# Hybrid attention layer on one core: the input turned by DMA transposes in place of fp32 transposes on TensorE

## The chip, the core and the metric

The kernel runs on one core of a Trainium2 chip. TensorE (PE in the profile) multiplies matrices, VectorE (DVE), ScalarE (ACT) and GpSimd (POOL) do elementwise work, and SyncE (SP) issues transfers to 16 DMA engines; ScalarE issues some as well. Every engine works through its own instructions in order. The metric is the time of one execution on the device in microseconds (us), lower is better.

## The reference

One decoder layer on 4096 tokens of width 1024, in fp32:

```
mod = silu(c) @ w_ada + b_ada;  shift, scale, gate = split(mod, 3)
h = rmsnorm(x, norm_g) * (1 + scale) + shift
proj = h @ w_in                       # 3328 columns, for two head groups
A: stick-breaking attention, 8 heads x 64, strictly causal, no softmax, SiLU gate
B: sliding window of 128, 8 query / 2 key-value heads x 64, ALiBi, sink logit, SiLU gate
x = x + gate * (concat(A, B) @ w_out);  out = rmsnorm(x, final_g)
```

## The kernel before

The tokens are taken in eight superblocks (s = 0 to 7) of 512, each of four blocks of 128. To keep fp32 accuracy with fp16 matmuls, every operand is split into a high and a low half, and every product takes three passes (high x high, high x low, low x high).

The normalised and modulated input of a superblock, hT, has the 1024 features on partitions, in eight groups k of 128, and the tokens as columns. A projection chunk (line 381) is 128 output columns for 512 tokens: 24 matmuls of 512 columns, written as four quarters of six. The values (lines 451 and 463) use hT as the stationary operand. In each superblock come first the sliding-window keys, four gates and four queries, the values, and the output projection of the superblock before (line 623); then, for each of four pairs of stick-breaking heads, chunks K, Q and G. The x items prepare hT of the next superblock while these twelve stick-breaking chunks run: x is loaded two blocks at a time, normalised (its square sum on ScalarE, line 304, the inverse root on GpSimd, the scaling on VectorE, line 309), and then turned on TensorE (`tr`, line 349): four items of four fp32 transposes into a PSUM buffer, evacuated by ScalarE with scale and shift (line 354), cast to the high half by VectorE (line 357), and the low half subtracted by GpSimd (line 358). The four PSUM buffers "mm" serve projections, output and these transposes in turn.

Attention runs in ticks laid between these items: a tick holds the scores z of a group of two query blocks and two heads (lines 493 to 500), or the products with the values, here called the value group (line 577) of the group two before. Between the two, ScalarE, VectorE and GpSimd make the weights (the stick-breaking scan is line 513), split them (lines 558 and 559), and SyncE turns them by DMA transposes (line 564). `gate` multiplies the result with the gate (line 593) and splits it (lines 594 and 595).

The order is written by hand. `main` fills a list of items with planned costs (1300 ns for a quarter), and each tick is placed by a due time worked out from these costs; `later(n, f)` runs f after n more items of TensorE's work. Items of cost 0 go between. In s = 0 the weights are loaded, split (lines 275 and 276) and written to DRAM for the later superblocks, and 22 extra items fold the gate into the output weights (lines 236 to 238), one after every second item.

Of the kernel before, what the change touches and what calls it, by code (L numbers as in the profile page):

```python
# [10 lines left out]
I32 = mybir.dt.int32  # L11
AF = mybir.ActivationFunctionType
# [4 lines left out]
D = 1024  # L17
# [19 lines left out]
class Ring:  # L37
    """n buffers of a tag, taken in turn"""
# [12 lines left out]
class Kern:  # L51
# [9 lines left out]
    def open_const(self, ctx):  # L61
# [66 lines left out]

    def mod_cols(self, which):
        nc = self.nc  # L130
        ps = self.P["pv"].tile([128, 512], F32, tag="pv", name="modps")
        for j in range(KD):
            nc.tensor.matmul(out=ps[:, j:j + 1], lhsT=self.fg[:, j * 128:(j + 1) * 128], rhs=self.ones[:, 0:1],
                             start=True, stop=True)
# [5 lines left out]
    def setup_x0(self):  # L140
        """modulation and the first superblock's input"""
# [7 lines left out]
        for t in xs[:2]:  # L149
            self.x_norm(t)  # L150
# [4 lines left out]
        for t in xs[2:]:  # L155
            self.x_norm(t)
# [18 lines left out]
        hT = self.hT[0] = self.P["hT"].tile([128, KD, 2, T], F16, tag="hT", name="hT")  # L175
        for k in range(KD):
            nc.scalar.activation(hT[:, k, 0, :], xT[:, k, :], AF.Identity, bias=self.s16[:, k:k + 1])
            nc.vector.scalar_tensor_tensor(out=hT[:, k, 1, :], in0=xT[:, k, :], scalar=self.s16[:, k:k + 1],
                                           in1=hT[:, k, 0, :], op0=ALU.add, op1=ALU.subtract)

    def setup_masks(self):
# [3 lines left out]
        rel = self.P["y32"].tile([128, 256], F32, tag="y32", name="rel")  # L185
# [7 lines left out]
        nc.gpsimd.memset(self.d1, 1.0)  # L193
        nc.gpsimd.affine_select(out=self.d1, in_=self.d1, pattern=[[0, 4], [1, 256]], compare_op=ALU.is_ge,
                                fill=0.0, base=-128, channel_multiplier=-1)

    def setup_wo_items(self):
        """gate folded into the output weights; every item loads for the one after next"""
# [15 lines left out]
        def bcast():  # L214
            gb = st["gb"] = self.fg
# [34 lines left out]
        return out + [(0.0, self.load_fg)]  # L250
# [77 lines left out]
    def x_items(self, s, row0):  # L328
# [8 lines left out]
        def norm(g):  # L337
            for b in (2 * g, 2 * g + 1):
                self.x_norm(st[b])
# [640 lines left out]
```

## Time and profile before

| | |
|---|---|
| time, median of 3 runs | 1821.07 us |
| lowest and highest | 1820.89 and 1821.63 us |
| span of the profiled execution | 1820.7 us |
| TensorE busy | 1711.4 us (94%) |
| VectorE, ScalarE, GpSimd busy | 1081.8, 768.6, 536.5 us |
| HBM read and written | 141.58 and 27.79 MB |

The span goes from the first to the last instruction of one profiled execution; it stands 0.4 us below the median time. Busy shares are means over the whole span. Matmuls are pipelined and their ends are modelled, so a TensorE shown as busy is not at its peak; the start times are what to compare.

### The profile page before, as it was taken

Reading aid. Unit: us, or ns where it says so; the run is one execution under the profiler, and the core shown is the slowest. Engines: PE = TensorE matmul, PEld = TensorE weight load, DVE = VectorE, ACT = ScalarE, POOL = GpSimd, SP = SyncE. Lnnn points to the kernel's source line nnn. Section 1 sums busy time; section 2 is a strip of 40 time slices with the busy share of each in tenths; the row PEclk is TensorE's granted clock in tenths of the full one; section 3 lists DMA queues with packets and bytes.
Section 4 is the critical chain, followed back from the end, with each engine's and each line's share of the span. In section 5 each row is a group of like instructions: output and inputs, shape, how many; then the busy total and the mean of one; then the engine's idle time right before and its main releaser. Section 6 shows DMA issues by size and latency. Waiting matters only on the chain.

```text
span 1820.7 us, 28484 instructions
## 1 busy us (share of the span) xinstructions
PE 1711.4 (94%) x10982; PEld 894.6 (49%) x10982; DVE 1081.8 (59%) x1888; ACT 768.6 (42%) x1476; POOL 536.5 (29%) x665
## 2 busy tenths in 40 slices
PE   3997689999999989999999999999899998999997
PEld 3453345444555444555455554545455544455443
DVE  5577872558635585365735567354863557546582
ACT  3544552445423453244524454243633445234441
POOL 2034440234312252133412343122531235212231
PEclk8998889999999999999999999999999999999999
DMA  8797652465526555256443565246552655426552
GB/s 288 215 243 198 182 157 72 116 170 160 135 54 145 172 151 135 59 151 188 132 99 91 146 187 143 59 125 187 143 147 56 141 172 144 127 64 152 154 118 85
DMA packets 361621, 257.85 MB, mean 142 GB/s; under 512 B 288604, under 2 KB 315268, under 8 KB 361476
## 3 DMA queue, kind: packets, MB, share of 16 engines
q1 hardware_dynamic: 340308, 178.86, 40.4%
q10 hardware_dynamic: 21168, 77.08, 12.6%
q8 instruction: 88, 1.44, 0.3%
q14 instruction: 57, 0.47, 0.1%
HBM read 141.58 MB, written 27.79 MB: 93 GB/s over the span
## 4 chain that ended last, share of the span: by engine, by line
PE 74%; DVE 14%; issue 4%; ACT 3%; POOL 2%; DMA 1%; ACTq 0%; DVEq 0%; POOLq 0%
PE mm L381 36%; PE mm L623 18%; PE mm L451 9%; PE pv L577 4%; PE z L500 3%; DVE nb L513 3%; PE mm L463 2%; DVE w L559 2%; DVE f L309 1%; DVE fg L124 1%; DVE beta L519 1%; POOL hT L358 1%; DMA wT<-w 1%; DVE w L276 1%; ACT w L558 1%
## 5 line engine op out<-in xcount | busy, mean ns | idle before, releaser
L381 PE MATMUL mm<-hT,w 128*128 128x512 f16 x4032 | 921.1, 384 | 9.7 <-ACT h L354 3.8
L381 PEld LDWEIGHTS <-w 128*128 128x128 f16 x4032 | 392.9, 99 | 471.3 <-issue 29.4
L623 PE MATMUL mm<-wo,yT 128*128 128x512 f16 x1536 | 347.1, 380 | 0.0
L549 POOL TENSOR_SCALAR p<-p,smm 128x256 f32<-128x256 f32 x256 | 122.5, 496 | 695.8 <-DVE smm L547 352.1
L623 PEld LDWEIGHTS <-yT 128*128 128x128 f16 x1536 | 148.6, 98 | 169.4 <-issue 1.3
L540 ACT ACTIVATE p<-sp,nm 128x256 f32<-128x256 f32 (+1 forms) x256 | 126.0, 493 | 214.1 <-DVE nm L533 214.1
L595 POOL TENSOR_TENSOR yT<-y,yT 128x256 f16<-128x256 f32 x128 | 144.5, 1129 | 235.9 <-DVE yT L594 200.3
L513 DVE TENSOR_TENSOR_SCAN nb<-nb,d 128x1024 f32<-128x1024 f32 x64 | 153.2, 2394 | 94.5 <-ACT nb L507 93.4
L509 POOL TENSOR_SCALAR_AFFINE_SELECT beta<-beta 128x512 f32<-128x512 f32 x64 | 108.3, 1692 | 242.1 <-ACT beta L508 242.1
L451 PE MATMUL mm<-wv,hT 128*128 128x512 f16 x768 | 172.5, 379 | 0.0
L533 DVE CUSTOM_DVE_ANT_0 sp<-z,bias,nsink 128x256 f32<-128x256 f32 (+1 forms) x256 | 107.3, 475 | 36.2 <-PE z L500 35.5
L559 DVE SCALAR_TENSOR_TENSOR w<-p,w 128x1024 f16<-128x1024 f32 x64 | 83.1, 1299 | 71.6 <-ACT w L558 71.6
L558 ACT ACTIVATE w<-beta 128x1024 f16<-128x1024 f32 x64 | 67.5, 1055 | 123.1 <-DVE beta L519 119.7
L451 PEld LDWEIGHTS <-hT 128*128 128x128 f16 x768 | 74.2, 98 | 84.3
L577 PEld LDWEIGHTS <-v 128*64 128x64 f16 x2304 | 89.0, 110 | 53.7 <-issue 49.8
L577 PE MATMUL pv<-wT,v 128*64 128x128 f16 (+1 forms) x2304 | 110.1, 240 | 1.8 <-DMA wT<-w 1.8
L507 ACT ACTIVATE nb<-z 128x1024 f32<-128x1024 f32 x64 | 65.4, 1022 | 98.7 <-PE z L500 73.2
L558 ACT ACTIVATE w<-p 128x1024 f16<-128x1024 f32 x64 | 67.6, 1057 | 83.4 <-POOL p L549 69.4
L304 ACT ACTIVATE junk<-f 128x1024 bf16<-128x1024 f32 x64 | 67.5, 1055 | 78.2 <-DVE f L629 63.8
L442 DVE SCALAR_TENSOR_TENSOR v<-mm,v 128x512 f16<-128x512 f32 (+1 forms) x64 | 31.3, 489 | 110.6 <-ACT v L441 109.0
L397 DVE SCALAR_TENSOR_TENSOR q<-mm,q 64x512 f16<-64x512 f32 x64 | 43.8, 684 | 80.1 <-ACT q L396 79.0
L559 DVE SCALAR_TENSOR_TENSOR w<-beta,w 128x1024 f16<-128x1024 f32 x64 | 83.0, 1297 | 6.6 <-ACT w L558 6.6
(105 smaller groups left out, 1727.8 us busy)
## 6 DMA issues: line engine op xcount, KB each, us to landing
w<-wsc ACTq DMA_DIRECT2D x147, 512.0 KB, 3.4
f<-in_x_dram SPq DMA_DIRECT2D x64, 512.0 KB, 3.9
q<-q SPq DMA_DIRECT2D x128, 128.0 KB, 2.6
out_dram<-f SPq DMA_DIRECT2D x32, 512.0 KB, 3.0
f<-in_w_in_dram SPq DMA_DIRECT2D x26, 512.0 KB, 5.4
wsc<-w SPq DMA_DIRECT2D x21, 512.0 KB, 4.6
wo<-in_w_ada_dram SPq DMA_DIRECT2D x16, 512.0 KB, 7.4
wT<-w SPq DMA_TRANSPOSE x256, 3.4
```

Of the source, the lines that this page charges most:

```text
L381: nc.tensor.matmul(out=ps, lhsT=w[:, k, a, :], rhs=hT[:, k, b, :], start=(k == 0 and i == 0), stop=(k == KD - 1 and i == 2))
L451: nc.tensor.matmul(out=ps, lhsT=hT[:, k, b, tb * 128:(tb + 1) * 128], rhs=self.wv[:, k, a, 0:512], start=(k == 0 and i == 0), stop=(k == K ...
L509: nc.gpsimd.affine_select(out=be[:, :, 128:256], in_=be[:, :, 128:256], pattern=[[0, 4], [-1, 128]], compare_op=ALU.is_ge, fill=0.0, base= ...
L513: nc.vector.tensor_tensor_scan(out=nbf, data0=nbf, data1=d1, initial=1.0, op0=ALU.mult, op1=ALU.max)
L533: nc.vector.tensor_tensor_reduce(out=sp[:, u, c0:256], in0=z[:, u, c0:256], in1=bias[:, c0:256], scale=-2.0 ** -(h + 1), scalar=self.nsink ...
L540: nc.scalar.activation(p[:, u, c0:256], sp[:, u, c0:256], AF.Exp, scale=-1.0, bias=nm[:, u:u + 1], accum_out=sm[:, u:u + 1])
L549: nc.gpsimd.tensor_scalar(out=p[:, u, :], in0=p[:, u, :], scalar1=sm[:, u:u + 1], scalar2=1.0, op0=ALU.mult, op1=ALU.mult)
L558: nc.scalar.activation(t[:, 0], w, AF.Copy, scale=WS)
L559: nc.vector.scalar_tensor_tensor(out=t[:, 1], in0=w, scalar=WS, in1=t[:, 0], op0=ALU.mult, op1=ALU.subtract)
L577: nc.tensor.matmul(out=pv[h * 64:(h + 1) * 64, o0:o0 + c1 - c0], lhsT=v[:, a, vc:vc + 64], rhs=wT[:, e, h, c0:c1], start=(n == 0 and i == ...
L595: nc.gpsimd.tensor_tensor(out=y[:, 1, cols], in0=y32, in1=y[:, 0, cols], op=ALU.subtract)
L623: nc.tensor.matmul(out=ps, lhsT=y[:, a, tb * 128:(tb + 1) * 128], rhs=self.wo[:, m, b, n * 512:(n + 1) * 512], start=(m == OORD[0] and i = ...
```

## The change

x of the next superblock now stays with tokens on partitions. A block is loaded, its square sum taken, and it is multiplied by the inverse root and by a row of modulation factors (VectorE), the row of shifts is added (GpSimd), and the result is split into a high half (ScalarE) and a low half (GpSimd) in a tile hl. Two DMA transposes then write both halves to hT, whose layout becomes block, half, feature group, token. The rows of factors and shifts are written to DRAM once and broadcast to all partitions for every superblock, into a pool of two buffers that the final-norm weights share; these are loaded anew for every superblock. The steps of the four blocks are placed after given chunks (`when`: load, norm, split for blocks 0 to 3, counted from the first stick-breaking chunk). The first superblock keeps its transposes on TensorE. Besides, the gate product is computed in place, gs has four buffers, the scan's mask is one byte per element, and the square sum's unused output goes into hT; the fourth sliding-window gate projection moves behind the second query projection, and in s = 0 the extra items begin before the values.

```diff
-        self.d1 = p.tile([128, 4, 256], BF16, name="d1")
+        self.d1 = p.tile([128, 4, 256], U8, name="d1")
         self.ones = p.tile([128, 1], F32, name="ones")
-        self.fg = p.tile([128, D], F32, name="fg")
+        self.arow = d.tile([1, D], F32, name="arow")
+        self.srow = d.tile([1, D], F32, name="srow")
...
-        acc = self.fg
+        acc = self.acc0
...
+    def bc(self, name):
+        return self.P["bc"].tile([128, D], F32, tag="bc", name=name)
...
-        hT = self.hT[0] = self.P["hT"].tile([128, KD, 2, T], F16, tag="hT", name="hT")
         for k in range(KD):
-            nc.scalar.activation(hT[:, k, 0, :], xT[:, k, :], AF.Identity, bias=self.s16[:, k:k + 1])
-            nc.vector.scalar_tensor_tensor(out=hT[:, k, 1, :], in0=xT[:, k, :], scalar=self.s16[:, k:k + 1],
-                                           in1=hT[:, k, 0, :], op0=ALU.add, op1=ALU.subtract)
+            xk = xT[:, k, :].rearrange("p (b t) -> p b t", t=128)
+            nc.scalar.activation(hT[:, :, 0, k, :], xk, AF.Identity, bias=self.s16[:, k:k + 1])
+            nc.vector.scalar_tensor_tensor(out=hT[:, :, 1, k, :], in0=xk, scalar=self.s16[:, k:k + 1],
+                                           in1=hT[:, :, 0, k, :], op0=ALU.add, op1=ALU.subtract)
+        for row, col in ((self.arow, self.a16), (self.srow, self.s16)):
+            nc.sync.dma_start(out=row.rearrange("o (k p) -> p (o k)", p=128), in_=col)
+
+    def new_hT(self, s):
+
+        self.hT[s] = self.P["hT"].tile([128, NB, 2, KD, 128], F16, tag="hT", name="hT")
+        return self.hT[s]
...
-        return out + [(0.0, self.load_fg)]
+        return out
...
     def load_fg(self):
+        self.fg = self.bc("fg")
         self.nc.sync.dma_start(out=self.fg, in_=self.final_g.unsqueeze(0).to_broadcast([128, D]))
...
+    def load_mod(self):
+        self.ab, self.sb = self.bc("ab"), self.bc("sb")
+        self.nc.sync.dma_start(out=self.ab, in_=self.arow.to_broadcast([128, D]))
+        self.nc.sync.dma_start(out=self.sb, in_=self.srow.to_broadcast([128, D]))
...
-    def ssq(self, xt):
-        junk = self.P["h32"].tile([128, D], BF16, tag="h32", name="junk")
+    def ssq(self, xt, junk):
+
+        junk = junk.rearrange("p k t -> p (k t)").bitcast(BF16)
...
-        def load(g):
-            for b in (2 * g, 2 * g + 1):
-                st[b] = self.x_load(self.x[bass.ds(row0 + b * 128, 128), :])
-
-        def norm(g):
-            for b in (2 * g, 2 * g + 1):
-                self.x_norm(st[b])
-
-        def tr(g, k):
...
-                    nc.tensor.transpose(ps[:, j * 256 + i * 128: j * 256 + (i + 1) * 128],
-                                        st[2 * g + i][:, kk * 128:(kk + 1) * 128], self.ident)
...
-                nc.scalar.activation(h[:, j, :], ps[:, j * 256:(j + 1) * 256], AF.Identity,
-                                     bias=self.s16[:, kk:kk + 1], scale=self.a16[:, kk:kk + 1])
-            cols = slice(g * 256, (g + 1) * 256)
-            nc.vector.tensor_copy(hT[:, k:k + 2, 0, cols], h)
-            nc.gpsimd.tensor_tensor(out=hT[:, k:k + 2, 1, cols], in0=h, in1=hT[:, k:k + 2, 0, cols], op=ALU.subtract)
...
+        def load(b):
+            if b == 0:
+                self.load_mod()
+            st[b] = self.x_load(self.x[bass.ds(row0 + b * 128, 128), :])
+
+        def norm(b):
+            xt = st[b]
+            r = self.ssq(xt, self.hT[s][:, b, 0])
+            self.later(2, lambda: modulate(xt, r))
+
+        def modulate(xt, r):
+            nc.vector.scalar_tensor_tensor(out=xt, in0=xt, scalar=r, in1=self.ab, op0=ALU.mult, op1=ALU.mult)
+            nc.gpsimd.tensor_tensor(out=xt, in0=xt, in1=self.sb, op=ALU.add)
+
+        def split(b):
+            xt = st.pop(b)
+            hl = self.P["hl"].tile([128, 2, D], F16, tag="hl", name="hl")
+            nc.scalar.activation(hl[:, 0], xt, AF.Copy)
+            nc.gpsimd.tensor_tensor(out=hl[:, 1], in0=xt, in1=hl[:, 0], op=ALU.subtract)
+            self.later(5, lambda: transpose(b, hl))
+
+        def transpose(b, hl):
+            for e in range(2):
+                nc.sync.dma_start_transpose(out=self.hT[s][:, b, e], in_=hl[:, e, :])
+
+        return [[(0.0, lambda f=f, b=b: f(b)) for f in (load, norm, split)] for b in range(NB)]
...
-                    nc.tensor.matmul(out=ps, lhsT=w[:, k, a, :], rhs=hT[:, k, b, :],
+                    nc.tensor.matmul(out=ps, lhsT=w[:, k, a, :], rhs=hT[:, :, b, k, :],
...
-                    nc.tensor.matmul(out=ps, lhsT=hT[:, k, b, tb * 128:(tb + 1) * 128], rhs=self.wv[:, k, a, 0:512],
+                    nc.tensor.matmul(out=ps, lhsT=hT[:, tb, b, k, :], rhs=self.wv[:, k, a, 0:512],
...
-        y32 = self.P["y32"].tile([128, 256], F32, tag="y32", name="y32")
-        nc.vector.tensor_tensor(out=y32, in0=pv, in1=self.g[(s, pair)][:, cols], op=ALU.mult)
+        y32 = self.g[(s, pair)][:, cols]
+        nc.vector.tensor_tensor(out=y32, in0=pv, in1=y32, op=ALU.mult)
...
-            r = self.ssq(xt)
+            r = self.ssq(xt, self.hT[s if self.general else min(s + 2, self.NS)][:, tb, 0])
...
-        order = [SWK] + [SWG + p for p in range(4)] + [SWQ + p for p in range(4)]
+        order = [SWK, SWG, SWG + 1, SWG + 2, SWQ, SWQ + 1, SWG + 3, SWQ + 2, SWQ + 3]
...
-        self.sorder = [SWK, SWG, SWG + 1, SWG + 2, SBV, SWG + 3, SBV + 1, SWQ, SBV + 2, SBV + 3, SWV] + order[6:]
+        self.sorder = [SWK, SWG, SWG + 1, SWG + 2, SBV, SWQ, SBV + 1, SWQ + 1, SBV + 2, SWG + 3, SBV + 3, SWV] + order[7:]
...
+            if s:
+                add([(0.0, lambda s=s: self.new_hT(s + 1))])
             add(self.chunk_items(s, SWK, self.evac_k(s, 4, "ksw")))
-            for p in range(4):
+            for p in range(3):
                 add(self.chunk_items(s, SWG + p, self.evac_g(s, 4 + p)))
             vi = self.v_items(s, s * NB)
             add(self.chunk_items(s, SWQ, self.evac_q(s, 4)))
             pair_groups(s, 4)
+            if s:
+                add([(0.0, self.load_fg)])
+            if s == 0:
+                extra += self.setup_wo_items()
...
-            if s == 0:
-                extra += self.setup_wo_items()
             for p in range(1, 4):
+                if p == 2:
+                    add(self.chunk_items(s, SWG + 3, self.evac_g(s, 7)))
                 add(self.chunk_items(s, SWQ + p, self.evac_q(s, 4 + p)))
...
+            xat = {}
+            when = ((1, 3, 5, 7), (2, 4, 6, 8), (3, 5, 7, 9)) if s else ((3, 4, 6, 8), (4, 6, 8, 9), (5, 7, 9, 10))
+            for b, its in enumerate(xi):
+                for i, it in enumerate(its):
+                    xat.setdefault(when[i][b], []).append(it)
+            if not xi:
+                add([(0.0, self.load_fg)])
             for p in range(4):
+                if s == 0 and p == 1:
+                    assert not extra
+                    add([(0.0, lambda: self.new_hT(1))])
...
-                    pg = p - (1 if s == 0 else 0)
-                    if xi and pg in (0, 1) and j == 2:
-                        add(xi[pg][0])
-                    if xi and pg in (1, 2) and j == 0:
-                        add(xi[pg - 1][1])
+                    add(xat.get(3 * p + j, []))
                 pair_groups(s, p)
-                if xi and pg in (1, 2):
-                    add(xi[pg - 1][2])
...
-BUFS = dict(f=4, hT=2, w=3, q=2, ksb=2, ksw=1, kp=1, v=5, nb=1, beta=1, w16=1, wT=2, gs=5, h32=2, y32=1, yT=12, sm=2,
+BUFS = dict(f=4, hT=2, w=3, q=2, ksb=2, ksw=1, kp=1, v=5, nb=1, beta=1, w16=1, wT=2, gs=4, hl=1, bc=2, yT=12, sm=2,
```

## Rows read from the trace of the kernel before

**Rows 1.** The page: span, and TensorE's busy time, share of the span, instructions.

```profile
span 1820.7 us, 28484 instructions
...
PE 1711.4 (94%) x10982; PEld 894.6 (49%) x10982; DVE 1081.8 (59%) x1888; ACT 768.6 (42%) x1476; POOL 536.5 (29%) x665
```

**Rows 2.** The page: chain that ended last, share of the span by engine.

```profile
PE 74%; DVE 14%; issue 4%; ACT 3%; POOL 2%; DMA 1%; ACTq 0%; DVEq 0%; POOLq 0%
```

**Rows 3.** Busy time in one superblock: length, each engine's us, clock, DMA share, GB/s.

```profile
460.00:675.00 215.00, 210.18 (x1370) 109.79 (x1368) 125.13 (x227) 91.37 (x180) 64.44 (x81) 0.99 0.51 132
```

**Rows 4.** TensorE in order of time: start, us, line, operation, count [idle before <-releaser].

```profile
1073.55 1.53 PE L349 MATMUL mm<-ident,f 128*128 128x128 f32 x12
...
1076.84 1.46 PE L381 MATMUL mm<-hT,w 128*128 128x512 f16 x6 [0.62 <-ACT h L354]
...
1095.91 1.47 PE L349 MATMUL mm<-ident,f 128*128 128x128 f32 x12
1101.01 1.12 PE L349 MATMUL mm<-ident,f 128*128 128x128 f32 x4 [3.63 <-DVE gs L426]
...
1104.34 0.28 PE L493 MATMUL z<-kp,q 128*128 128x128 f16 x2
```

**Rows 5.** Busy time in other stretches: stick-breaking, transposes, first superblock and its transposes.

```profile
1042.88:1105.39 62.51, 57.77 (x363) 30.75 (x362) 44.56 (x55) 34.00 (x53) 27.42 (x25) 0.97 0.65 172
1095.90:1104.34 8.44, 4.81 (x23) 2.99 (x22) 5.72 (x10) 4.94 (x10) 3.15 (x4) 0.80 0.36 68
44.35:261.99 217.64, 182.12 (x1094) 92.69 (x1093) 161.47 (x253) 116.28 (x205) 73.28 (x79) 0.89 0.75 204
221.89:235.36 13.47, 5.57 (x25) 2.99 (x23) 12.31 (x16) 7.99 (x12) 4.98 (x4) 0.69 0.77 179
254.04:261.99 7.95, 5.10 (x24) 2.95 (x22) 4.82 (x8) 5.38 (x10) 3.59 (x4) 0.73 0.35 66
```

**Rows 6.** Pieces of the chain in order of time: start us, us, what.

```profile
307.95 4.02 PE mm L463 x72
...
1042.88 15.65 PE mm L381 x72
```

**Rows 7.** Groups by line: engine, operation, count | busy us, mean ns | idle before.

```profile
L381 PE MATMUL mm<-hT,w 128*128 128x512 f16 x4032 | 921.1, 384 | 9.7 <-ACT h L354 3.8 <-ACT hT L177 2.3 <-DVE w L276 2.2
...
L358 POOL TENSOR_TENSOR hT<-h,hT 128x512 f16<-128x512 f32 x56 | 73.7, 1325 | 29.4 <-DVE hT L357 29.4
...
L354 ACT ACTIVATE h<-mm,s,a 128x256 f32<-128x256 f32 x112 | 55.4, 561 | 24.6 <-POOL hT L358 23.3
...
L610 DVE SCALAR_TENSOR_TENSOR f<-f,r,fg 128x1024 f32<-128x1024 f32 x32 | 41.4, 1294 | 35.8 <-POOL r L293 35.7
...
L357 DVE CAST hT<-h 128x512 f16<-128x512 f32 x56 | 31.5, 581 | 39.0 <-ACT h L354 39.0
...
L238 POOL TENSOR_TENSOR wo<-xT,wo 128x1024 f16<-128x1024 f32 x8 | 17.0, 2129 | 17.7 <-ACT wo L237 17.7
...
L237 ACT ACTIVATE wo<-xT 128x1024 f16<-128x1024 f32 x8 | 8.5, 1057 | 26.2 <-DVE xT L236 26.1
```

**Rows 8.** Instructions on tile wT: duration ns min/median/max; time to landing.

```profile
L564 SPq DMA_TRANSPOSE wT<-w x256: 1231/1250/5056, 93.8 to 1773.1; - x128
...
DMA to landing us min/median/max: 3.0/3.4/9.6
```

**Rows 9.** DMA queues from 918 to 924 us: share of 16 engines.

```profile
q1 hardware_dynamic: 2112, 0.52, 45.2%
```

**Rows 10.** In order of time: a value group, and the transposes split in its tick.

```profile
1084.29 0.85 PE L577 MATMUL pv<-wT,v 128*64 128x256 f16 x18
1088.67 3.49 SPq L564 DMA_TRANSPOSE wT<-w  x2
```

**Rows 11.** Lines L595 and L513: duration ns min/median/max, first and last start.

```profile
L595 POOL TENSOR_TENSOR yT<-y,yT x128: 663/1512/1652, 116.9 to 1788.8; 128x256 f16<-128x256 f32 x128
...
L513 DVE TENSOR_TENSOR_SCAN nb<-nb,d x64: 2276/2292/3407, 177.7 to 1766.7; 128x1024 f32<-128x1024 f32 x64
```

More of the change, by code (lines that the diff above doesn't have):

```diff
@@ L11 @@
 I32 = mybir.dt.int32
+U8 = mybir.dt.uint8
 AF = mybir.ActivationFunctionType
@@ L132, in mod_cols @@
         for j in range(KD):
-            nc.tensor.matmul(out=ps[:, j:j + 1], lhsT=self.fg[:, j * 128:(j + 1) * 128], rhs=self.ones[:, 0:1],
+            nc.tensor.matmul(out=ps[:, j:j + 1], lhsT=self.acc0[:, j * 128:(j + 1) * 128], rhs=self.ones[:, 0:1],
                              start=True, stop=True)
@@ L148, in setup_x0 @@
         xT = self.P["hT"].tile([128, KD, T], F32, tag="hT", name="xT")
-        for t in xs[:2]:
-            self.x_norm(t)
+        hT = self.new_hT(0)
+        for b in range(2):
+            self.x_norm(xs[b], hT[:, b, 0])
         self.run_later(9)
@@ L154, in setup_x0 @@
             self.mod_load(0, k, stage[:, k])
-        for t in xs[2:]:
-            self.x_norm(t)
+        for b in range(2, NB):
+            self.x_norm(xs[b], hT[:, b, 0])
         self.run_later(9)
@@ L192, in setup_masks @@
                                 fill=NEG, base=-1, channel_multiplier=-1)
-        nc.gpsimd.memset(self.d1, 1.0)
-        nc.gpsimd.affine_select(out=self.d1, in_=self.d1, pattern=[[0, 4], [1, 256]], compare_op=ALU.is_ge,
+        d1 = self.P["beta"].tile([128, 4, 256], F32, tag="beta", name="d1f")
+        nc.gpsimd.memset(d1, 1.0)
+        nc.gpsimd.affine_select(out=d1, in_=d1, pattern=[[0, 4], [1, 256]], compare_op=ALU.is_ge,
                                 fill=0.0, base=-128, channel_multiplier=-1)
+        nc.vector.tensor_copy(self.d1, d1)
     def setup_wo_items(self):
@@ L214, in bcast @@
         def bcast():
-            gb = st["gb"] = self.fg
+            gb = st["gb"] = self.acc0
             for k in range(KD):
@@ L360, in x_items @@
-        out = []
-        for g in range(2):
-            out.append(([(0.0, lambda g=g: load(g))], [(0.0, lambda g=g: norm(g))],
-                        [(440.0, lambda g=g, k=k: tr(g, k)) for k in range(0, KD, 2)]))
-        return out
+        def load(b):
[6 more added lines that the diff above has]
+            self.later(2, lambda: modulate(xt, r))
@@ L462, in shared @@
                 for i, (b, a) in enumerate(PASSES):
-                    nc.tensor.matmul(out=ps, lhsT=hT[:, k, b, tb * 128:(tb + 1) * 128], rhs=self.wv[:, k, a, 512:640],
+                    nc.tensor.matmul(out=ps, lhsT=hT[:, tb, b, k, :], rhs=self.wv[:, k, a, 512:640],
                                      start=(k == 0 and i == 0), stop=(k == KD - 1 and i == 2))
@@ L664, in main @@
         self.vready, self.deferred = {-1}, []
+        self.acc0 = self.bc("acc0")
         self.setup_small()
@@ L898, in attend @@
                     self.att_s3("G", pair, g, st, 0)
-            for g in self.x_items("G", row0):
-                for it in g:
-                    run(it)
+            self.new_hT("G")
+            for its in self.x_items("G", row0):
+                run(its)
             self.v[-1] = vprev
```

19 lines of the change are left out of this document (5 added, 14 removed).

## The prediction

> **What bounds the kernel now.** I read the page's totals first, then the chain that ended last, then busy time over one repeating stretch, then TensorE's instructions in order of time. The totals show TensorE busy for 1711.4 us of 1820.7 [rows 1], and the chain runs through it for 74% of the span [rows 2]. Neither says whether what is removed is worth anything, since busy time is modelled and the chain mixes stages. The steady stretch does: a superblock takes 215 us, TensorE is idle for 4.8 us of it, and granted clock is 0.99, practically the 2.4 GHz level [rows 3]. TensorE's own rows show where that idle time lies: matmuls follow one another without a pause except at the two groups of x transposes at L349 [rows 4]. So every instruction taken off TensorE there shortens the superblock, and so does every wait. The first superblock is another stage: 217.6 us, of which TensorE is busy for 182.1, at a mean clock of 0.89 [rows 5], because weights are still being split on ScalarE and VectorE.
>
> **What is removed.** The first group of 16 transposes starts at 1073.55 and the next chunk's matmul at 1076.84: 3.29 us. The second starts at 1095.91, and the scores that follow six chunk matmuls start at 1104.34: 8.43 us [rows 4]. Six chunk matmuls at full clock are 6 x 15.65 / 72 = 1.30 us [rows 6], so the second group costs 7.13. The transposes themselves are short there. The time is the wait of 3.63 us for a PSUM buffer, which VectorE frees late (L426), and what follows: over this stretch the granted clock is 0.80, a mixture of both levels, and the four transposes and six matmuls after the wait last 3.33 us [rows 4, 5]. Together 3.29 + 7.13 = 10.42 us for each superblock; six of them (s = 1 to 6) give 62.5 us. In s = 0 the same two groups take 13.47 and 7.95 us, each with six matmuls in it [rows 5]: 13.47 + 7.95 - 2.60 = 18.8. Sum removed: 81.3 us.
>
> **What is added to the other engines.** Per superblock ScalarE loses 16 evacuations of 561 ns (9.0 us) and gains four casts of about 1.06 (4.2). VectorE loses eight casts of 581 ns and four scalings, and gains four two-tensor products like L610, 1.29 each. GpSimd loses eight subtractions of 1.33 us (10.6) and gains four additions and four subtractions of 1024 columns; the nearest row is L238's 2.13 [rows 7], so 17.0 us. VectorE and GpSimd are busy for 44.6 and 27.4 us of the 62.5 us in which all this happens [rows 5], so I cost it at nothing; TensorE's matmuls are the cover, and if it is gone the price is in the rivals.
>
> **What the new path costs.** Eight more DMA transposes run per superblock, of the form that the kernel already uses for the attention weights: 1.25 us on SyncE's queue, 3.4 us to landing in the median and 9.6 at most [rows 8]. Two of them took 45.2% of six microseconds on the queue that carries little else there, about 1.36 us each [rows 9]: 10.9 us more per superblock. In the stick-breaking stretch the DMA share is 0.65 [rows 5], 40.6 us; with eight transposes and two 512 KB broadcasts it comes to some 0.85 to 0.9 of a shorter stretch. It is not the bound, but landing becomes later.
>
> What is late next is the fourth block. Its modulation is issued eleven chunk quarters before the next superblock's first matmul, which reads all four blocks. Eleven quarters of 6 x 0.217 are 14.3 us; two scores and two value groups at about 0.85 (the value group's row is in [rows 10]) make 17.7. The chain is product 1.29, addition 2.13, cast 1.06, subtraction 2.13, second transpose's issue 1.25 and landing 3.4: 11.3 us. The slack of 6.4 is eaten by queues: SyncE issued the weights' transposes 4.4 us after the value group that goes with them [rows 10], because it waits for VectorE in order, and the new transposes stand behind the copies of q, which wait for VectorE too. GpSimd's work also has the mask of the scores in between. With two such delays, 8.8, the block is 2.4 us late. Bounds: 0, and 8.6 if it lands after 9.6 instead of 3.4 us. I take 2 us for each of six superblocks, nearest to the median: -12.
>
> In s = 0 the fourth block's split follows one chunk after the third's, hl has one buffer, and the third block's transposes come just behind that split. ScalarE so holds until they have landed, about 7 us after the chunk; cast, subtraction, issue and landing add 7.8, and TensorE gets there about 6.9 us after that chunk (four quarters, a score and a value group). Wait: 7 + 7.8 - 6.9 = 7.9, so -8 (bounds 0 and 12).
>
> **Moved and small parts.** Folding the gate into the output weights starts twelve quarters earlier in s = 0. TensorE's idle time there is 35.5 us, of which 10.7 belongs to the transposes [rows 5]; the other 24.8 can shrink or grow, as those steps now meet sliding-window attention instead of the scans. I take 0, with +15 and -20 as ends. The gate is computed in place, so a gs buffer is held until GpSimd's L595 and there are four instead of five. The buffer of a superblock's third gate projection is freed only by the value group one quarter before; ScalarE may wait some microseconds for it, but four PSUM banks keep TensorE going, three chunks of 5.2 us. The scan's mask changes type and the final-norm weights are reloaded: nothing, behind the matmuls. The moving operand becomes four runs of 128 columns. No row shows such a read. If each run cost as a separate 128-column matmul, 4.02 / 72 = 0.0558 us [rows 6], four would take 0.223 instead of 0.217, 24 us over L381's 4032 [rows 7]; I take 0, since it stays one instruction, and keep 24 as the far end.
>
> **Sum.** 81.3 - 12 - 8 + 0 = 61.3; 1820.7 - 61.3 = 1759 us. The profiled span and the median of the runs (1821.07) differ by 0.4 us, so I make no correction.
>
> **Rivals.**
> (a) Everything is hidden: no wait at the superblock's end. 1820.7 - 81.3 = 1739. For it speaks the 6.4 us of slack, against it the queue delays. If the first superblock's idle time shrinks too, about 1725.
> (b) The port that VectorE and GpSimd contend for becomes the limit. GpSimd's 256-column subtraction takes 0.66 us at least but 1.51 in the median, and the scan 2.28 at least and 3.41 at most [rows 11]; both lengthen when they meet. If the 17.0 - 10.6 = 6.4 us that GpSimd gains all delay VectorE and through it the fourth block, six superblocks lose 38 us more: 1759 + 38 = 1797. For it: in this stretch the two engines' busy times add up to 72.0 of 62.5 us [rows 5]. Against it: VectorE's lag can run on into the projections that follow.
> The Trainium skill, page "SBUF — State Buffer", section "SBUF: two separate sides", calls the pair an exclusive lock, held for a whole instruction by VectorE with two SBUF inputs or by GpSimd; the lengthened rows agree with it, and by that rule the time would be 1797 if VectorE were the bound.
> (c) Slower than before: the fourth block's transposes land so late that each superblock loses more than the 10.4 us it gained. After an idle time of 3.63 us the next ten instructions took 3.33 us instead of about 1.7, so a wait of 9 us costs about 10.5. That point is reached when chain and queues take 26.7 us instead of 17.7. At 12 us per wait plus 1.6, six superblocks lose 82 and s = 0 its 12: 1820.7 - 81.3 + 82 + 12 = 1833. For it speaks only the largest landing of 9.6 us.
> The Trainium skill, page "VectorE: DVE Perf Modes", section "Rules for kernel authors", advises TensorE for a 128x128 transpose whose result may go to PSUM and the DMA crossbar otherwise, with 1309 ns for one by DMA. By that figure 64 tiles would be an estimated 84 us of DMA per superblock. The trace does not agree: eight tiles occupy the engines for 1.36 us.
> (d) The gain is mostly given back or never there (waits of 6 us, s = 0 wins nothing): 62.5 - 6 x 6 = 26, so 1794.
>
> **Chances.** Forecast (1745 to 1773) 0.57; (a) 0.17; (b) and (d) together 0.17; (c) 0.05; no difference 0.04. Range 1734 to 1796, from (a) to (b), which leaves out the fast end of (a) and (c). A difference below 0.2% (3.6 us) counts as none, the three runs before lie within 0.04%. Faster 0.91, same 0.04, slower 0.05.
>
> **What would show it.** Steady superblocks of 205 to 208 us, no L349, TensorE idle only just before a superblock's first chunk, there released by a DMA transpose. Long waits of ScalarE or SyncE for GpSimd would speak for (b), TensorE clocks below 0.95 in the steady part for (c) or (d). The forecast fails if superblocks stay near 215, if chunk matmuls take more than 0.217, or if s = 0 grows beyond its 217.6.

## The result and the profile after

The changed kernel takes 1869.07 us (median of four runs, 1866.72 to 1876.51) against 1820.98: a ratio of 1.027 (95% interval 1.0249 to 1.0291), slower by 48 us where 1759 us was forecast. The page of its trace, beside [rows 1, 2]:

```profile
span 1869.4 us, 28003 instructions
...
PE 1703.5 (91%) x10758; PEld 871.6 (47%) x10758; DVE 1120.5 (60%) x1833; ACT 762.1 (41%) x1408; POOL 627.4 (34%) x665
...
PE 63%; DVE 14%; POOL 6%; DMA 6%; issue 5%; ACT 4%; SPq 2%; ACTq 0%; POOLq 0%; DVEq 0%
```

The transposes are gone, yet TensorE's busy time fell by only 8 us, though they had 34.3 us of it (L349): the chunk matmuls, L397 now, are shown with 938.6 us instead of L381's 921.1 [rows 7], as matmuls behind a wait last longer (17 take 5.41 us at 934.45 below, where 18 take 4.06). Its share of the chain fell from 74% to 63%, and GpSimd and DMA took it over: something that was beside TensorE's work now stands in front of it. To see where, take one mark in every superblock, the start of the first stick-breaking key chunk. TensorE in order of time, superblocks 1 and 7:

```profile
412.48 1.90 PE L397 MATMUL mm<-hT,w 128*128 128x512 f16 x8
...
1736.89 1.90 PE L397 MATMUL mm<-hT,w 128*128 128x512 f16 x8
```

Before, the same chunks start at 397.62 and 1687.95. So superblock 1 is 14.9 us late, and the six steady superblocks take 220.7 us each instead of 215.1. From superblock 7 on nothing more is lost. Without any transposes on TensorE a superblock would take 215.06 - 10.42 = 204.6; so in each some 16 us go to new waits and to slower matmuls behind them. Busy time in four stretches, columns as in [rows 3]: a superblock, its stick-breaking part, the end of that part, and superblock 0 up to superblock 1.

```profile
745.90:965.20 219.30, 208.70 (x1337) 106.54 (x1336) 130.28 (x218) 90.11 (x170) 77.09 (x80) 0.98 0.60 146
856.00:934.40 78.40, 67.85 (x422) 33.88 (x421) 61.25 (x60) 37.72 (x49) 44.17 (x28) 0.96 0.86 203
927.10:939.70 12.60, 5.90 (x23) 2.21 (x19) 7.44 (x9) 2.39 (x3) 2.53 (x3) 0.73 0.83 178
44.35:273.60 229.25, 178.92 (x1056) 88.43 (x1055) 164.88 (x241) 113.74 (x194) 88.13 (x79) 0.87 0.77 205
```

DMA share is 0.86 in the stick-breaking part, as the forecast had it, and TensorE is idle for 10.6 us of 78.4, where [rows 5] has 4.7 of 62.5, most of it at the transposes (to the end of the part, 1042.88 to 1120.82, it is 4.7 of 77.9). Superblock 0 up to the first chunk of superblock 1 now takes 229.25 us, with 50.3 idle; before, that chunk started at 259.13, 14.5 us sooner. The end of the part is the costliest place. TensorE there, columns as in [rows 4]:

```profile
904.14 4.06 PE L397 MATMUL mm<-hT,w 128*128 128x512 f16 x18
...
910.31 0.23 PE L509 MATMUL z<-kp,q 128*128 128x128 f16 x1 [2.05 <-DMA q<-q]
...
917.57 4.06 PE L397 MATMUL mm<-hT,w 128*128 128x512 f16 x18
921.46 1.04 PE L516 MATMUL z<-ksb,q 128*128 128x256 f16 x8
...
926.32 0.85 PE L593 MATMUL pv<-wT,v 128*64 128x256 f16 x18
932.86 0.59 PE L397 MATMUL mm<-hT,w 128*128 128x512 f16 x1 [5.70 <-DMA hT<-hl]
934.45 5.41 PE L397 MATMUL mm<-hT,w 128*128 128x512 f16 x17 [1.00 <-DMA hT<-hl]
939.70 0.28 PE L509 MATMUL z<-kp,q 128*128 128x128 f16 x2
```

From the value group's end to the next scores, 18 matmuls take 12.6 us instead of 3.9: 6.7 us are waits for the fourth block's DMA transposes, and 2 more pass at a mean granted clock of 0.73 behind them. So the place costs 8.7 us. Over the whole span TensorE waits like this (us in total, times, longest):

```profile
PE mm L397 <- DMA hT<-hl: 56.3, 14, 12.8
PE z L509 <- DMA q<-q: 29.6, 12, 6.9
```

The longest of the first kind, 12.8, is the one in front of superblock 1. There ScalarE's cast of the fourth block had itself waited 12.77 us, until the third block's transposes had landed and so freed the one hl tile. In the steady part, how the fourth block came so late is in the chain that ended last, followed from 863 to 936 (start us, us, what). The pieces are of all three later blocks; TensorE is in it only at its end.

```profile
863.11 6.34 DMA f<-in_x_dram
...
872.94 4.25 POOL f L367
...
893.49 4.02 DVE nb L529
...
907.11 3.31 DVE nb L529
...
913.56 1.58 POOL yT L611
...
917.46 4.25 POOL f L367
...
926.92 0.68 DVE q L413
927.63 0.70 DVE q L415
928.34 0.44 SPq L425
928.87 0.55 SPq L426
...
930.93 3.48 DMA hT<-hl
934.45 1.86 PE mm L397 x4
```

Instructions of SyncE, ScalarE and VectorE in that time, in the order of their starts:

```profile
906.99 0.54 SPq L425 DMA_DIRECT2D q<-q  x1
908.22 0.59 SPq L319 DMA_DIRECT2D f<-in_x_dram  x1
913.09 1.04 ACT L326 ACTIVATE hT<-f 128x1024 bf16<-128x1024 f32 x1
916.08 1.28 DVE L366 SCALAR_TENSOR_TENSOR f<-f,r,ab 128x1024 f32<-128x1024 f32 x1 [1.47 <-POOL r L314]
```

Read it from the end. SyncE issues the block's transposes at 929.47 only because they stand behind the copies of q, which wait for VectorE's L415. VectorE is late there because of what GpSimd does beside it: the addition L367 takes 4.25 us next to a scan (2.36 in the median), VectorE's L534 behind the scan takes 2.12 us (0.17 at 930.89, without an addition beside it), and the mask L525, for which VectorE's L535 waits, stands behind the addition (rows in the last section). Further back, scans of 4.02 and 3.31 us (2.28 at least, [rows 11]) stand in front of VectorE's short work, both next to subtractions on GpSimd. The addition itself comes at 917.46, right behind its product on VectorE (916.08), and the product waited for the inverse root r, which GpSimd makes after L611 from a square that ScalarE began at 913.09; the block's load was issued at 908.22, behind copies of q. The engines and SyncE's queue pass one late piece on to the next, each in order.

### The profile page after: what moved, and what is told of

It is laid out like the page before. It is cut to its first block, busy times and chain, and to the rows that moved or that the text cites. A ratio compares the mean times of both kernels' runs of the same rounds, so it can differ in the third digit from the quotient of the medians.

```text
span 1869.4 us, 28003 instructions
## 1 busy us (share of the span) xinstructions
PE 1703.5 (91%) x10758; PEld 871.6 (47%) x10758; DVE 1120.5 (60%) x1833; ACT 762.1 (41%) x1408; POOL 627.4 (34%) x665
## 4 chain that ended last, share of the span: by engine, by line
PE 63%; DVE 14%; POOL 6%; DMA 6%; issue 5%; ACT 4%; SPq 2%; ACTq 0%; POOLq 0%; DVEq 0%
PE mm L397 27%; PE mm L639 18%; PE mm L467 8%; POOL f L367 3%; PE pv L593 3%; DVE nb L529 3%; PE z L516 3%; PE mm L479 2%; DMA hT<-hl 2%; DMA f<-in_x_dram 2%; DVE w L575 1%; DVE acc L126 1%; DVE f L366 1%; DVE w L291 1%; DVE q L415 1%
## 5 line engine op out<-in xcount | busy, mean ns | idle before, releaser
L397 PE MATMUL mm<-hT,w 128*128 128x512 f16 x4032 | 938.6, 389 | 64.5 <-DMA hT<-hl 56.3
L397 PEld LDWEIGHTS <-w 128*128 128x128 f16 x4032 | 395.4, 100 | 542.2 <-issue 96.6
L611 POOL TENSOR_TENSOR yT<-gs,yT 128x256 f16<-128x256 f32 x128 | 162.6, 1270 | 210.3 <-DVE yT L610 175.8
L529 DVE TENSOR_TENSOR_SCAN nb<-nb,d 128x1024 f32<-128x1024 f32 x64 | 166.9, 2607 | 109.3 <-ACT nb L523 108.8
L556 ACT ACTIVATE p<-sp,nm 128x256 f32<-128x256 f32 (+1 forms) x256 | 126.0, 493 | 204.6 <-DVE nm L549 204.4
L525 POOL TENSOR_SCALAR_AFFINE_SELECT beta<-beta 128x512 f32<-128x512 f32 x64 | 102.1, 1596 | 137.9 <-ACT beta L524 137.9
L326 ACT ACTIVATE hT<-f 128x1024 bf16<-128x1024 f32 x64 | 67.5, 1055 | 111.3 <-DVE f L645 63.5
L367 POOL TENSOR_TENSOR f<-f,sb 128x1024 f32<-128x1024 f32 x28 | 90.6, 3236 | 56.0 <-DVE f L366 56.0
L516 PEld LDWEIGHTS <-q 128*128 128x128 f16 x768 | 71.6, 100 | 30.9 <-DVE nm L549 9.2
```

The costliest lines, as they stand in the source:

```text
L367: nc.gpsimd.tensor_tensor(out=xt, in0=xt, in1=self.sb, op=ALU.add)
L397: nc.tensor.matmul(out=ps, lhsT=w[:, k, a, :], rhs=hT[:, :, b, k, :], start=(k == 0 and i == 0), stop=(k == KD - 1 and i == 2))
L516: nc.tensor.matmul(out=o, lhsT=q[:, j, h, cols], rhs=kt[:, kh, (qb - 1) * 128:(qb + 1) * 128], start=(j == 0), stop=(j == 1))
L529: nc.vector.tensor_tensor_scan(out=nbf, data0=nbf, data1=d1, initial=1.0, op0=ALU.mult, op1=ALU.max)
L556: nc.scalar.activation(p[:, u, c0:256], sp[:, u, c0:256], AF.Exp, scale=-1.0, bias=nm[:, u:u + 1], accum_out=sm[:, u:u + 1])
L611: nc.gpsimd.tensor_tensor(out=y[:, 1, cols], in0=y32, in1=y[:, 0, cols], op=ALU.subtract)
```

## Experiments

Times are medians, each with its ratio to the kernel before on the same chip. "A superblock" is the mean distance of the first value matmuls in superblocks 1 to 7; the kernel before has 215.1, the changed one 220.7, and 204.6 is the aim. It comes from one trace of each; e7's is of a run 12 us below its median and e2's of one 4.5 above, the others lie within 3.5. Two theories stood at the outset: P, only the fourth block's place is wrong; C, the stick-breaking part is crowded on the engines beside TensorE.

**e1_free_hT: TensorE never waits for a turned block** (superblocks 1 to 7 read superblock 0's tile, so their right input is left out).

```diff
+    def read_hT(self, s):
+        return self.hT[s if self.general else 0]
...
-            w, hT, ps = self.wq[(s, c)], self.hT[s], st["ps"]
+            w, hT, ps = self.wq[(s, c)], self.read_hT(s), st["ps"]
```

> Edit: from the second superblock on the projections read the h tile of the first superblock, so TensorE never waits for a DMA transpose; every load, split and transpose is still made, into the other buffer. It leaves out the right input of superblocks 1 to 7. Theory P (place): what was lost is the wait for the fourth block's transposes at the end of each superblock, 8.7 us with the slow clock behind it, six times, and 16 us in front of superblock 1; taking it away gives 1869 - 52 - 16 = 1801 us. Theory C (crowd): in the stick-breaking part the in-order queues of VectorE, GpSimd and SyncE carry more than that stretch holds, and the wait at the end is only where their lateness shows; without it the same queues are late in the next stretch (q copies, hidden-layer scans, gates), so less than half of the 68 us comes back: 1835 to 1855 us.

Measured 1812.65 us (0.9956, 0.9939 to 0.9972), 56 less than the changed kernel, nearer to P. A superblock takes 211.5: the waits for hT cost 9.2, in agreement with the 8.7 read above. But 6.9 over 204.6 stays, so C holds for the rest. In front of superblock 1 much less comes back than the 13.8 us waited there (12.8 and 1.0): its first value matmul starts at 301.4 instead of 306.2, since ScalarE still waits 12.77 us for the hl tile and TensorE's next scores then wait 7.3 us until ScalarE, late by that, has made beta from the scores before (the longest wait of the second row):

```profile
PE z L514 <- DMA q<-q: 33.0, 15, 6.7
PE z L514 <- ACT beta L529: 17.2, 7, 7.3
```

**e14_fourth_only: only the fourth block one chunk earlier**, and **e3_one_earlier: all four blocks one chunk earlier** (in superblocks 1 to 6, which prepare 2 to 7; in `when` the rows are load, square and split, the columns the blocks).

```diff
-            when = ((1, 3, 5, 7), (2, 4, 6, 8), (3, 5, 7, 9)) if s else ...
+            when = ((1, 3, 5, 6), (2, 4, 6, 7), (3, 5, 7, 8)) if s else ...    # e14
+            when = ((0, 2, 4, 6), (1, 3, 5, 7), (2, 4, 6, 8)) if s else ...    # e3
```

> Edit: the changed kernel with nothing but the fourth x block of superblocks 1 to 7 one chunk earlier (load, square and split); the other three blocks stay where the change put them. If it is the fourth block's turns alone that TensorE waits for at the superblock's end, this wins all that freeing the h tile won, 9.2 us a superblock: 1869 - 55 = 1814 us. If the blocks hold one another up (one split tile and in-order queues between them), the fourth cannot come a whole chunk earlier and the gain is less than half: 1840 to 1869 us.

> Edit: in superblocks 1 to 7 the load, the square and the split of each x block are put one chunk (some 9 us of TensorE's order) earlier. Theory P: the wait of 5.7 us and more in front of the next superblock goes, 6 x 8.7 = 52 us: 1817 us. Theory C: the same work meets the same queues one chunk earlier and the waits come back as waits for q copies and scans: 1850 to 1869 us.

e14: 1823.57 us (1.0023, 1.0011 to 1.0035), a superblock 212.5. One block's place carries 8.2 us a superblock, nearly all that e1 freed, and it brings back 45 of the 48 us that the change lost; the 13.8 us that are still waited for turned blocks all lie in front of superblock 1. e3: 1803.13 us (0.99, 0.9883 to 0.9916), a superblock 208.8: more than P allowed. With all blocks earlier the hT waits shrink to the one in front of superblock 1, and the q waits become many and short:

```profile
PE z L509 <- DMA q<-q: 30.7, 22, 6.8
...
PE mm L397 <- DMA hT<-hl: 14.8, 3, 14.1
```

**e11_two_earlier: blocks 1 to 3 yet one chunk earlier.** By P this should have changed nothing. (It and the next one also have superblock 0's x blocks one chunk earlier.)

```diff
-            when = ((0, 2, 4, 6), (1, 3, 5, 7), (2, 4, 6, 8)) if s else ...
+            when = ((0, 1, 3, 5), (1, 2, 4, 6), (2, 3, 5, 7)) if s else ...
```

> Edit: all x blocks one chunk earlier, and in superblocks 1 to 7 blocks 1 to 3 one chunk earlier again. By theory P the turns are no longer waited for in these superblocks, so an earlier place wins nothing more: 1798 us within 4. If the place still costs (transposes in front of the q copies on SyncE), the time moves by more than 4 us either way.

1827.53 us (1.0043, 1.0029 to 1.0058) against e6's 1798.44; a superblock 213.6. No turned block is waited for in the steady part, and still 4.7 us are lost. In one stick-breaking part TensorE waits:

```profile
856.87 0.22 PE L509 MATMUL z<-kp,q 128*128 128x128 f16 x1 [0.64 <-DMA q<-q]
...
877.82 0.22 PE L509 MATMUL z<-kp,q 128*128 128x128 f16 x1 [1.72 <-DMA q<-q]
...
888.40 1.47 PE L397 MATMUL mm<-hT,w 128*128 128x512 f16 x6 [2.22 <-DMA w<-wsc]
...
902.01 0.22 PE L509 MATMUL z<-kp,q 128*128 128x128 f16 x1 [2.56 <-DMA q<-q]
```

So P alone falls: earlier is not better by itself. Blocks 0 and 1 now follow each other one chunk apart, not two, and the kernel's own work behind them comes late. That the bunching is the cause is the reading of the trace; an even spread two chunks earlier was not tried.

**e6_all_earlier: superblock 0's blocks one chunk earlier as well.**

```diff
-            when = ((1, 3, 5, 7), (2, 4, 6, 8), (3, 5, 7, 9)) if s else ((3, 4, 6, 8), (4, 6, 8, 9), (5, 7, 9, 10))
+            when = ((0, 2, 4, 6), (1, 3, 5, 7), (2, 4, 6, 8)) if s else ((2, 3, 5, 7), (3, 5, 7, 8), (4, 6, 8, 9))
```

> Edit: as the kernel with x one chunk earlier in superblocks 1 to 7 (1803 us), and the x blocks that superblock 0 prepares one chunk earlier too. Theory P (place): the wait of 14.1 us in front of superblock 1 is the fourth block's place again; one chunk (12 us) earlier leaves 2 us of it: 1803 - 12 = 1791 us. Rival: in superblock 0 the x blocks share the four f buffers and SyncE's queue with the loads of w_in, and an earlier x load makes the weights late by as much as it wins: 1800 to 1806 us.

1798.44 us (0.9879, 0.9863 to 0.9896), between the two cases: the wait in front of superblock 1 only falls from 14.1 to 9.8. That the weights' loads and splits, which share buffers and queues with x there, hold it up is what was expected; no run shows it by itself.

**e7_no_add and e4_add_dve: GpSimd's addition left out** (with it the shift of x in superblocks 1 to 7, so their right input), **or moved to VectorE**, both on the changed kernel.

```diff
-            nc.gpsimd.tensor_tensor(out=xt, in0=xt, in1=self.sb, op=ALU.add)
+            nc.vector.tensor_tensor(out=xt, in0=xt, in1=self.sb, op=ALU.add)    # e4; e7: no line
```

> Edit: the changed kernel without GpSimd's addition of the shift row; it leaves the shift out of x from the second superblock on, places are as in the changed kernel. If GpSimd's work is what makes the blocks late (2.36 us an addition, 4.26 us where it meets VectorE's scan, and ScalarE's cast waiting 79.5 us in 25 waits for it), the wait at the superblock's end falls from 5.7 us to about 2 and the six superblocks win 4 to 8 us each: 1820 to 1845 us. If only the place counts, GpSimd's part was hidden, as the prediction had it: 1864 to 1870 us.

> Edit: the changed kernel with the addition of the shift row on VectorE in place of GpSimd. If GpSimd's slow pass is what makes the blocks late, VectorE adds in about 1.3 us what GpSimd adds in 2.4 to 4.3, and the scan loses its neighbour: 1835 to 1855 us. If VectorE is the engine short of time in the stick-breaking part, 28 more passes of 1.3 us on it make it slower: 1870 to 1900 us.

e7: 1847.63 us (1.0152, 1.0135 to 1.0169), 21 less than the changed kernel, 3.6 a superblock; its trace, of a faster run, has superblocks of 215.4, 5.3 less. GpSimd's part was not hidden, but not where e7 expected it: behind the first superblock (from 310 us on) TensorE's waits for turned blocks stay (44.9 us, 42.5 in the changed kernel), and its waits for q nearly go (1.9 us, from 18.6). So what the addition costs shows at the copies of q, and without it the fourth block is still waited for. e4: 1872.36 us (1.0274, 1.0257 to 1.0291): equal within 4 us to the changed kernel, although the addition takes 1.23 us there; the waits for turned blocks are 62.9 us in all (56.3).

**e10_early_add_dve: the same edit where the place is right** (on e6).

> Edit: all x blocks one chunk earlier (1798 us), with the shift's addition on VectorE in place of GpSimd. On the changed kernel itself this edit moved nothing (1872 against 1869). If GpSimd's passes (4.26 us beside the scan, with the masking of beta queued behind them and VectorE's cast of y taking 1.55 to 2.20 us beside them, 0.29 otherwise) cost time in the stick-breaking part, it wins 5 to 25 us. If both engines have the room, it gives 1798 us within 4. If VectorE is the tighter of the two, 1803 to 1815 us.

1792.43 us (0.9835, 0.9818 to 0.9852) against e6's 0.9879, intervals apart: 6 us faster, and a superblock of 208.2 instead of 208.9. VectorE's groups in e6 first, then in e10:

```profile
L529 DVE TENSOR_TENSOR_SCAN nb<-nb,d 128x1024 f32<-128x1024 f32 x64 | 174.5, 2727 | 67.5 <-ACT nb L523 67.0
...
L610 DVE CAST yT<-gs 128x256 f16<-128x256 f32 x128 | 63.8, 498 | 4.4
```

```profile
L529 DVE TENSOR_TENSOR_SCAN nb<-nb,d 128x1024 f32<-128x1024 f32 x64 | 161.2, 2519 | 49.9 <-ACT nb L523 49.3
...
L610 DVE CAST yT<-gs 128x256 f16<-128x256 f32 x128 | 41.5, 324 | 4.4
```

Without GpSimd's addition beside them, VectorE's scan and cast shorten by 13 and 22 us in all, which pays for the 28 additions that VectorE takes over (35.5 us). ScalarE's cast also waits less for the addition, 37.5 us instead of 82.9. Which of the two gives the 6 us is not separated.

**e9_lag: the scores' lag 3500 instead of 3000 ns** (on e6, one constant).

> Edit: all x blocks one chunk earlier (1798 us), and the planner's lag for a pair of stick-breaking heads 3500 ns in place of 3000, so that their score matmuls come later behind the q chunk. In the trace of all earlier, TensorE's only waits left in a steady superblock are four of 0.25 to 1.7 us for the q copies, 3.9 us together, and the superblock takes 209.0 us where 204.6 without transposes was to be had. If the q copies' lateness is what is left, it gives up to 6 x 3 us: 1780 to 1790 us. If the later scores only make the weights of the attention late in turn, 1798 us or more.

1797.83 us (0.9882, 0.9866 to 0.9897): no difference. The waits for q stay 27.0 us in 23 (27.8 in 22).

**e8_x_in_proj: x prepared in the projection part**, where VectorE and GpSimd are nearly idle. An earlier form, e5_x_in_proj, let the output blocks' squares write their discarded product over the next superblock's filled h tile, so its input was lost and the kernel's own flag sent it through its general path: 10459.58 us, which tells nothing of the theories. In e8 these squares write into the hl tile.

```diff
+            add_x()                                  # after SWK, the gates, SWQ and each value block
...
-                    add(xat.get(3 * p + j, []))
+                    add(xat.get(3 * p + j, []) if s == 0 else [])
```

> Edit: in superblocks 1 to 6 the x blocks of the next superblock are loaded, modulated, split and turned in the projection part of the superblock (between the shared key and gate chunks and the value blocks), where VectorE and GpSimd are nearly idle (17% and 5% of 942.88 to 988 in the trace before), and none of it stands in the stick-breaking part; superblock 0 stays as it is in the changed kernel. Theory P: the wait at the end goes, 52 us: 1817 us. Theory C: the six steady superblocks fall from 220.7 us to what they have without any transposes on TensorE, 215.1 - 10.4 = 204.6: 1869 - 6 x 16 = 1773 us, and waits in the stick-breaking part go as well as those at its end.

> Edit: superblock 0 as in the kernel that has all x blocks one chunk earlier; in superblocks 1 to 6 the x blocks of the next one are prepared in the projection part (shared key to values), where VectorE and GpSimd are nearly idle, and none of it stands in the stick-breaking part; the output blocks' squares write their discarded product into the split's tile, since the h tile is filled by then. If the stick-breaking part is crowded by this work (q copies behind turns on SyncE, scans beside GpSimd), the superblock falls from 208.8 us to the 204.6 that TensorE alone needs: 25 us less than all earlier, 1766 to 1780 us. If the place alone was the fault, one chunk earlier has already taken it all and this gives the same as all earlier, within 5 us.

1931.31 us (1.0602, 1.0585 to 1.062): both cases missed by far. ScalarE and then TensorE in one superblock:

```profile
830.04 1.06 ACT L372 ACTIVATE hl<-f 128x1024 f16<-128x1024 f32 x1 [14.14 <-DMA hT<-hl]
```

```profile
832.96 0.29 PE L509 MATMUL z<-kp,q 128*128 128x128 f16 x1 [14.06 <-DVE q L413]
```

There is one hl tile. ScalarE's next cast waits until the last block's transposes have landed; those stand on SyncE's queue behind the attention weights' transposes; and behind the cast stands the evacuation of q, for which TensorE waits, six times and 85.0 us in all. Two hl tiles were not tried. Idle engines don't help if an in-order wait stands in front of what TensorE needs.

**e2_moves_only, e12_s0_pe, e13_s0_before: superblock 0.** e2 takes x the old way everywhere and keeps all moves. e12 is e10 with the old turning in superblock 0 alone (its fp32 half product goes into hl). e13 is e12 with superblock 0's old order of chunks, weights and w_out items.

```diff
+            xp = self.x_items_pe(s + 1, (s + 1) * T) if s == 0 else []     # e12: transposes on TensorE
...
-            for p in range(3):                                              # e13
+            for p in range(3 if s else 4):
```

> Edit: x goes the old way (normalised, fp32 transposes on TensorE, scale and shift on ScalarE, cast on VectorE, subtraction on GpSimd), everything else that the change moved is kept: the new order in superblock 0, the early wo items, the tile layout with the strided moving operand, one buffer more for gs, the in-place gate. If the moves cost nothing, as the prediction had it, this gives 1821 us, within 5. If the loss of 14.5 us in superblock 0 comes from the moves (weights that are needed earlier), it gives 1833 to 1840. If the strided moving operand costs (far end of the prediction), it gives up to 1845.

> Edit: x one chunk earlier and the addition on VectorE (1792 us), but superblock 0 turns the blocks of superblock 1 by fp32 transposes on TensorE, as the kernel before does, at that kernel's places. If in superblock 0, where weights are loaded and split through the same buffers and queues, turning by DMA costs more than TensorE's transposes (11.7 us late at superblock 1 in the trace of the kernel with the addition on VectorE, 4.3 us in that of the moves alone), it wins 7 us: 1785 us. If the 11.7 us come from elsewhere, 1792 us or, with TensorE's transposes added to the waits, up to 1811.

> Edit: as the kernel whose superblock 0 turns on TensorE, and superblock 0 also takes its chunks, its weights and the items of w_out in the order of the kernel before. If the moves in superblock 0 cost the 4.3 us that the moves alone showed, it wins those: 1781 us against 1785. If they cost nothing, the two are equal within 2 us.

e2: 1825.34 us (1.0024, 1.0014 to 1.0034); superblocks of 215.5, so layout and moves cost nothing there. e12: 1778.77 us (0.9765, 0.9753 to 0.9778), the fastest of all. e13: 1781.39 us (0.9792, 0.9779 to 0.9805), no faster: the premise that the old order wins 4 us falls. The first value matmul of superblock 1 comes at 306.2 in the changed kernel, 303.1 in e10, 295.7 in e2, 293.4 in e12 and 296.6 in e13; before, where the values stand one chunk later in the order, it came at an equivalent of 291.4 (306.2 - 14.9, by the mark). So in superblock 0 turning by DMA costs 10 us more than the transposes on TensorE (303.1 - 293.4). The 2 to 5 us by which e12, e2 and e13 still come later than before can't be put down to the new order, since e13 has the old one and is the latest of the three; what causes them stays open, and single traces differ by as much. TensorE's waits up to 310 us show what stands in place of the transposes: for copies of q 11.0 us in the changed kernel against 3.7 in e2, for ScalarE's beta 6.6 against none, and for turned blocks 13.8. The steady superblocks of e12 take 207.3 us in the mean (208.2 in e10, with the same order; why is not shown). One of them, and what is left of TensorE's waits for q:

```profile
707.40:914.40 207.00, 205.09 (x1338) 105.56 (x1337) 131.03 (x222) 90.33 (x170) 63.76 (x76) 1.00 0.64 155
```

```profile
PE z L551 <- DMA q<-q: 17.2, 20, 2.9
```

## Why the prediction was wrong

The forecast missed by 110 us. A steady superblock was to take 215.1 - 10.4 + 2 = 206.7 and took 220.7: 84 us over six. Superblock 0 was to win 18.8 - 8 = 10.8 and lost 14.9: 26 us.

- *What is removed, 10.4 us a superblock and 18.8 in superblock 0.* In the steady part this was nearly right: e12's 207.3 us are within 3 us of 204.6, so at least 7.8 of the 10.4 can be had. In superblock 0 no run that turns by DMA there had the 18.8: other waits, for copies of q and for ScalarE's beta, came in the transposes' place. That the weights' loads and splits are behind them is not shown; for the weights themselves TensorE waits only some 6 us there.
- *The fourth block, "the slack of 17.7 against a chain of 11.3 and two queue delays of 4.4".* This is the step that failed. The chain with its delays was well sized in its sum: from the product's start at 916.08 to the landing at 934.45 it took 18.4 us, forecast 20.1. In its parts that was luck: the queue behind the copies of q took 3.9 us where two delays made 8.8, and the addition 4.25 where 2.13 was put. The slack was not: the product starts 11.0 us before TensorE needs the block (927.1), not 17.7. The slack counted from the place of the product in the program, and TensorE passed that place at about 905.4 (behind the first of the three quarters that start at 904.14). VectorE got to it only when r was there, after a load that SyncE issued at 908.22 and a square that ScalarE began at 913.09, both behind other work. So the block was 7.4 us late instead of 2.4, and with the low clock this cost 8.7. (The forecast's bounds, 0 and 8.6, hold the 7.4, but for a late landing, not for a late start.) e1 puts it at 9.2, e14 shows that it is the fourth block's place, and e3 that with all blocks one chunk earlier it is gone.
- *"VectorE and GpSimd are busy for 44.6 and 27.4 us of the 62.5, so I cost it at nothing; TensorE's matmuls are the cover".* Failed too: the other 6.9 us a superblock, which stay in e1. The cover was a sum of busy times, and the work was a chain of short steps over four in-order engines, on the same engines that bring q and the weights to TensorE. e7 shows GpSimd's part in it (waits for q of 1.9 us instead of 18.6), and the same places with all blocks earlier leave 4.2 (e3), with the addition on VectorE 3.6 (e10). e11 and e8 show that the sum of busy times says nothing of what a wait stands in front of. How much of it comes from DMA engines that are fuller (x's load lands after 4.4 us in the median, 3.9 before) and how much from the order on the queues, no run separates.
- *Wait in superblock 0, -8.* The mechanism was right, the one hl tile at which ScalarE holds; the size was not: ScalarE waited 12.77 us there and got to the fourth block's cast at 268.73, some 15 us behind that chunk and not 7, so that TensorE's wait was 13.8 (12.8 + 1.0). Its price is not 13.8, though: freed of it, e1 gets only 4.8 us back, as ScalarE's other work is late with it. The "moves" at 0 were nearly right (e2: 4.4 us over the whole kernel), the strided moving operand at 0 right: 18 matmuls from 917.57 to 921.46 are 0.216 us each, as before.
- *Rival (c)* named the right place, and 9 us as its point of no gain. It got 0.05 because only landing times were held to speak for it: landing is 4.2 us in the median now, and lateness came from the queues ahead. Its sign, a clock below 0.95 in the steady part, did not come: the superblock shows 0.98. The range reached to (b), and (b)'s 6.4 us of GpSimd work a superblock is not far from what e7 gave back (3.6 to 5.3), but it shows at the copies of q, on top of the wait for the fourth block and not through it.

## What to carry to other kernels

Measure slack from when the engine will reach an instruction, not from where the program puts it: take the last wait on each of its inputs in the trace before, and add what stands ahead on every queue that the chain passes. Work moved from the bounding engine to idle ones is free only if none of its waits stands ahead of something the bounding engine needs; its place then matters more than its price (one chunk for one block was worth 45 us here, and one chunk more for three blocks cost 29). Where the new way costs more than it frees, as in superblock 0, keep the old way there: e12 does, and is 2.3% faster than the kernel before.

## What the runs showed of the hardware

VectorE and GpSimd don't slow each other evenly: one waits until the other's instruction ends. VectorE and GpSimd in order of time in the changed kernel:

```profile
917.28 2.28 DVE L529 TENSOR_TENSOR_SCAN nb<-nb,d 128x1024 f32<-128x1024 f32 x1
917.45 4.26 POOL L367 TENSOR_TENSOR f<-f,sb 128x1024 f32<-128x1024 f32 x1 [1.40 <-DVE f L366]
...
919.60 2.12 DVE L534 TENSOR_TENSOR alive<-alive,nb 128x4 f32<-128x4 f32 x1
921.66 0.63 POOL L525 TENSOR_SCALAR_AFFINE_SELECT beta<-beta 128x512 f32<-128x512 f32 x1
```

The scan came first and took its 2.28 us; the addition (2.36 us in the median of L367) took 4.26, longer by most of the scan; then a maximum over four columns (L534, 0.41 us in the median, 0.17 at least) took 2.12, until the addition's end at 921.7. The Trainium skill, page "SBUF — State Buffer", section "SBUF: two separate sides", says just this of the port pair that the two engines share: whoever starts first keeps it for the whole instruction and the other blocks. The trace agrees, in these rows. By itself it decided little: e4 took the addition off GpSimd and moved nothing, and e10 won 6 us.
